# Two-operand vector work of GpSimd moved to VectorE in a transformer block

## The chip, the cores and the metric

The kernel runs on one core of a Trainium2 chip. A core has five engines that run their own queues of instructions in order and wait for each other by semaphores: TensorE (in the profile PE for its matmuls and PEld for its weight loads), VectorE (DVE), ScalarE (ACT), GpSimd (POOL) and SyncE (SP), which here only issues DMAs. The metric is the device time of one execution in microseconds (us); less is better.

## The reference

One layer of a hybrid encoder on a sequence of 1024 rows with 1024 features, in f32. A token mixer runs a short convolution and an attention without softmax side by side, merges them under two gates, and a squared-ReLU MLP of 4096 features follows.

```python
mod = c @ w_ada[l] + b_ada[l]
sh1, sc1, gt1, sh2, sc2, gt2 = jnp.split(mod, N_MOD, axis=-1)
h = modulate(rms_norm(x, g_pre_mix[l]), sh1, sc1)
proj = h @ w_in[l]
bg, cg, u, q, k, v, ga, gb = jnp.split(proj, split_pts, axis=-1)
y_conv = short_conv_branch(bg, cg, u, conv_w[l]) @ w_proj_conv[l]
o = stick_breaking_attention(q, k, v)       # 8 heads of 64
y_attn = o @ w_proj_attn[l]
merged = jax.nn.sigmoid(ga) * y_conv + jax.nn.sigmoid(gb) * y_attn
x = x + gt1[:, None, :] * rms_norm(merged @ w_out[l], g_post_mix[l])
h2 = modulate(rms_norm(x, g_pre_mlp[l]), sh2, sc2)
ff = jnp.square(jax.nn.relu(h2 @ w_mlp_in[l])) @ w_mlp_out[l]
x = x + gt2[:, None, :] * rms_norm(ff, g_post_mlp[l])
```

The attention weight of row t on row s < t is sigmoid(z_ts) times the product of 1 - sigmoid(z_tj) over the rows j between s and t: a running product from the diagonal to the left.

## The kernel before

**Numbers in two parts.** Every f32 operand of a large matmul is written as the sum of two numbers of a shorter type (fp32r), a high part and a low part. `split` (L101) makes them: ScalarE copies the operand into the high part, which rounds it (L103), and `sub` (L89, L90) subtracts the high part from the operand, on VectorE or on the engine that is handed in. A product is then three matmuls: high by high, high by low, low by high.

**Products of pairs.** The gates, both products of the MLP and their operands go through a seven-product scheme for 2 by 2 blocks (`pair_products`, L222, with the order 1, 2, 6, 5, 7, 3, 4 of L161). It needs sums and differences of the four blocks of each operand. For weights `side_s` (L163) makes four of them per pair of output columns, all on GpSimd, called from `pair_factors` (L207) with `nc.gpsimd` at L216; `parts` then splits each operand with VectorE for the low part. For activations the four blocks are turned into each other in place, step by step (L806 to L821 for the gates, `second_half`, L1099, for the MLP's first product).

**The stages**, in the order of time:

- The prologue (L373 to L536): x is normalised and turned, a part of the modulation and the value columns are computed. `value_rows` (L467) splits the 8 rows of the value weights with the low part on GpSimd.
- Attention and convolution (L552 to L788). For 8 heads and 4 pairs of row blocks, `weights_of` (L659) computes two sigmoids of the scores on ScalarE, clears the upper triangle of the diagonal block on GpSimd (L685), runs the product from the right as a scan on VectorE (L689), and multiplies both (L693). That multiplication is on GpSimd for the row blocks 0, 1, 2, 4 and 6 (widths 128, 256, 384, 640 and 896 columns) and on VectorE for 3, 5 and 7. `attend` (L702) then turns the weights on TensorE (L719), splits them (ScalarE and VectorE, tile `tu`) and multiplies by the values (L730); `finish` adds two halves (L740, tile `ot`). Between these, the projections for q, k and the convolution fill TensorE's time (L546); a string (L765) gives TensorE's order by hand: n for a step of weights, w for one of attending, f for one of filling.
- The gates (L794 to L897): operand sums over both parts of h, on an engine for each instruction by a string of p and v (L804), then 8 pairs of products with evictions on VectorE (L852) while the rest of the modulation is accumulated (L144).
- The two branch products (L962, L1001). `merged` (L983) multiplies by a gate on VectorE and adds the other branch on GpSimd (16 times, L986, by the string MERGED), then splits.
- The output product with residual and norms by blocks of 128 rows (L1042), with each block's columns turned and scaled into the MLP's operand. The last block's sums and low parts (`second_half`) follow an order string at L1229 in which a p sends an instruction to GpSimd: 15 of them.
- The MLP's first product: 16 pairs, `pair_products` with four weight sums each on GpSimd; results go to DRAM (`f_d`).
- The MLP's second product (L1266 to L1370): five groups of 2, 4, 4, 4 and 2 blocks, each with seven steps. `make` (L1186) forms a step's sums and both parts, two steps ahead of its matmuls (L1285): the sums of the weight side (64 in all) and the low parts of the weight side for odd blocks (56) on GpSimd, the rest on VectorE. `gather` (L1290) adds each result from PSUM into `ffacc` on VectorE (L1295). `finish_half` (L1329) scales the finished halves by a gain, 12 of 16 times on GpSimd, takes the norm, adds the residual and stores.

**The order.** In the prologue TensorE's and SyncE's queues, and in the attention TensorE's, are in the order of the code. All other queues are ordered by a planner when the program is built: it takes instructions as their inputs become ready by its own costs and prefers those that stand earlier in the code. Once built, each queue runs in order: an instruction that waits holds up what is behind it. SyncE issues all loads and stores.

Other work of GpSimd, which is not touched: memsets (among them L671), the powers -1/2 in `rstd_of` (L131), and the triangle (L685).

Of the kernel before, what the change touches and what calls it, by code (L numbers as in the profile page):

```python
# [30 lines left out]
def block_kernel(  # L31
# [19 lines left out]
    nc = tc.nc  # L51
# [132 lines left out]
    def sums_t(quads, i, k, eng=nc.vector):  # L184


        (q11, q12), (q21, q22) = quads[k]
        if i == 6:
            sub(q11, q12, q11, eng)
            sub(q12, q22, q12, nc.gpsimd)  # L190
            sub(q22, q22, q11, eng)
        else:
            sub(q21, q21, q22, nc.gpsimd)
# [13 lines left out]
    def pair_factors(raw, new_f, new_r):  # L207


        xs = {1: raw[0][:, :, :P], 2: raw[1][:, :, :P]}  # L210

        def split_of(i):
            if i not in xs:
                xs.update(side_s(
                    raw[0][:, :, :P], raw[1][:, :, :P], raw[0][:, :, P:], raw[1][:, :, P:],
                    new_f, nc.gpsimd,  # L216
                ))
            return parts(xs[i], lambda: new_r(i), nc.vector)

        return split_of  # L220
# [152 lines left out]
    with ExitStack() as es:  # L373
# [93 lines left out]
        def value_rows(k, n):  # L467
            raw = stage((P, n, CW))
            nc.sync.dma_start(
                raw, w_in[k * P : (k + n) * P, v0 : v0 + CW].rearrange("(a p) n -> p a n", p=P)  # L470
            )
            for i in range(n):
                hi, lo = wv[k + i] = tuple(
                    st.tile([P, CW], F32R, name=f"wv{w}{k + i}") for w in "hl"
                )
                split(raw[:, i, :], hi, lo, nc.vector if k + i in WV_DVE else nc.gpsimd)
# [43 lines left out]
        WV_DVE = set()  # L520
# [31 lines left out]
    with ExitStack() as es:  # L552
# [48 lines left out]
        def conv_taps(k):  # L601
            u = cv.tile([P, T + 2], F32, tag="cu", name=nm("cu"), bufs=1)
            y = uy[k]
            nc.gpsimd.memset(u[:, 0:2], 0.0)

            def use(half, ps):
                s = halves[half]
                nc.vector.tensor_tensor(
                    u[:, s.start + 2 : s.stop + 2], ps, y[:, s], op=ALU.mult
                )  # L610
                (nc.gpsimd if k in TAP else nc.vector).tensor_scalar(
                    y[:, s], u[:, s.start : s.stop], taps[:, k, 0:1], None, op0=ALU.mult
                )
                for j in (1, 2):
                    nc.vector.scalar_tensor_tensor(
                        y[:, s], u[:, s.start + j : s.stop + j], taps[:, k, j : j + 1], y[:, s],
                        op0=ALU.mult, op1=ALU.add,
                    )

            return use  # L620
# [38 lines left out]
        def weights_of(hd, i, out):  # L659
# [12 lines left out]
            for s0 in range(0, w, HALF):  # L672
# [11 lines left out]
                if s1 == w:  # L684
# [8 lines left out]
                    (nc.gpsimd if i in MUL else nc.vector).tensor_tensor(  # L693
# [65 lines left out]
        MUL = (0, 1, 2, 4, 6)  # L759
        TAP = ()  # L760
# [33 lines left out]
    with ExitStack() as es:  # L794
# [7 lines left out]


        engines = "pppvvpvpvpvp pvvpvppvpppv pvpvvvvppvpv vvpvvvvpvvpv"  # L804
        gate_on = on(engines)
        for k in range(4):  # L806
            q11, q12, q22, q21 = (gt.tile([P, HALF], F32, tag="e", name=nm("e"), bufs=8) for _ in range(4))
            quads.append([[q11, q12], [q21, q22]])
            for o, i, eng in zip((q11, q12, q22, q21), (1, 5, 3, 2), gate_on[k]):
                hi, lo = yop[i][k]  # L810
                add(o, f(hi), f(lo), eng)
            for (o, l, r), eng in zip(
                ((q11, q12, q11), (q12, q22, q12), (q22, q22, q11), (q21, q21, q22)), gate_on[k][4:]
            ):
                sub(o, l, r, eng)
            for i, eng in zip((6, 7, 4), gate_on[k][8:]):
                split_t(quads, yop, i, k, eng=eng)
        for _ in fill:
            pass
        for k in range(4):  # L820
            split_t(quads, yop, 5, k, eng=gate_on[k][11])  # L821
# [126 lines left out]
    MERGED = "pppppppppppppppp vvvvvvvvvvvvvvvv"  # L948
# [79 lines left out]
    with ExitStack() as es:  # L1028
# [70 lines left out]
        def second_half(step):  # L1099
# [4 lines left out]
            eng = nc.gpsimd if "p" in rest else nc.vector  # L1104
# [81 lines left out]
    def make(n):  # L1186

        g, i = steps[n]
        for j in range(GROUPS[g]):
            for side, o, a, b, op in SUMS.get(i, ()):  # L1190
                eng = nc.gpsimd if side == "x" else nc.vector
                o, a, b = (raw_of(r, j, side) for r in (o, a, b))
                eng.tensor_tensor(o, a, b, op=op)
        made[n] = []
        for j in range(GROUPS[g]):
            fs = []
            for side in "xy":
                to = factor_at(n, j, side)
                eng = nc.gpsimd if side == "x" and j % 2 else nc.vector
                split(raw_of(WHERE[side][i], j, side), *to, eng)  # L1200
# [25 lines left out]
    with ExitStack() as es:  # L1226
        def rest_of_h():
            order = """
                53ap 50a s50ap 51a 52a s51a n0 n1 51b 50b s52a s31 s30 52b 53b s53a 73ap 72ap 70p s33 s53b 60 s50b s52bp s32 71p 72bp 62p 73bp s51b 63 61 42p s62p 41p s63 s60 40a s42 s71 s61 43 40b s40p s70 s73 s43 s72p s41  # L1229
# [36 lines left out]
    with ExitStack() as es:  # L1266
# [56 lines left out]


        GAIN = "pppv pppv pppv pppv"
        SUM = "vvvv vvvv vvvv vvvv"
        AT = {(0, 0): 0, (1, 1): 1, (1, 0): 2, (0, 1): 3}

        def finish_half(b, q):  # L1329
# [14 lines left out]
            eng = nc.vector if GAIN.split()[b % 4][AT[b // 4, q]] == "v" else nc.gpsimd  # L1344
            eng.tensor_tensor(o, o, g2r[q], op=ALU.mult)
            if again:
                r = rstd_of(ss)
                for h in range(2):
                    o = acc[:, b, halves[h]]
                    if SUM.split()[b % 4][AT[b // 4, h]] == "v":  # L1350
                        nc.vector.scalar_tensor_tensor(
                            xt[h], o, r, xt[h], op0=ALU.mult, op1=ALU.add
                        )
                    else:
                        nc.scalar.activation(o, o, AF.Copy, scale=r)
                        add(xt[h], xt[h], o, nc.gpsimd)
# [46 lines left out]
```

## Time and profile before

| | |
|---|---|
| time, median of 3 runs | 1512.68 us |
| all runs | 1512.03, 1512.68, 1515.39 us |
| the profiled execution, its own time | 1514.89 us |
| its span, first to last instruction | 1513.2 us |
| mean granted TensorE clock | 0.968 |

The span is the time from the first to the last instruction that the profiler recorded; the little that the execution's own time has on top lies around it. In rows of the trace an instruction is named by engine, line, operation and out<-in of the tiles; a line can be that of a helper (L90 is every `sub`), so the tile names tell where it belongs: `y`, `g`, `h`, `fr` are slots of the MLP, `e`, `gy` and `t`, `s` the gates' operands and weights, `a` and `pt` the attention's weights, `cy` and `cu` the convolution's. "x78 | 79.5, 1058" means 78 instructions, 79.5 us busy in all, 1058 ns each on average; after it stands how long the engine idled just before them and which instruction ended that. Records of VectorE overlap a little, since the next one starts before the last one's record ends; the pace is read from start to start.

### The profile page before, as it was taken

How to read it: one execution, taken by the hardware profiler on the slowest of the kernel's cores; microseconds unless marked ns; L12 is line 12 of the kernel's file. 1: busy time of each engine (PE TensorE's matmuls, PEld its weight loads, DVE VectorE, ACT ScalarE, POOL GpSimd, SP SyncE). 2: the span in 40 equal slices, each digit the busy share in tenths (PEclk: the TensorE clock that was granted, in tenths of full speed). 3: DMA queues.
4: the chain of work that ended last, by engine and by line, in shares of the span. 5: the costliest groups of instructions: out<-in, count | busy, mean ns of one | idle time of the engine just before them, and what ended most of it. 6: DMA issues, size and time to landing. Idle time of an engine off the chain costs nothing.

```text
span 1513.2 us, 18030 instructions
## 1 busy us (share of the span) xinstructions
PE 1394.2 (92%) x6281; PEld 1131.0 (75%) x6281; DVE 1090.9 (72%) x1355; ACT 643.8 (43%) x1301; POOL 598.7 (40%) x516
## 2 busy tenths in 40 slices
PE   5999999999967998999999699999999699999976
PEld 4788778888855876788787478888887478787865
DVE  6737877877699665347546966555536988989988
ACT  5646656656324433413355433333323443343532
POOL 3214434434384332005104643333314645748365
PEclk9999999999988999999999799999999899999998
DMA  8501011111125566654413133333355225150224
GB/s 299 161 28 34 23 50 48 29 57 28 57 70 153 186 222 219 211 195 148 142 70 112 56 112 112 112 112 112 112 181 179 93 64 166 57 167 29 84 70 167
DMA packets 107567, 171.10 MB, mean 113 GB/s; under 512 B 7322, under 2 KB 66766, under 8 KB 107476
## 3 DMA queue, kind: packets, MB, share of 16 engines
q1 hardware_dynamic: 107476, 169.95, 34.2%
q8 instruction: 49, 0.80, 0.2%
q14 instruction: 42, 0.34, 0.1%
HBM read 132.16 MB, written 37.76 MB: 112 GB/s over the span
## 4 chain that ended last, share of the span: by engine, by line
PE 63%; DVE 19%; DMA 6%; issue 5%; ACT 4%; POOL 3%; SPq 0%; DVEq 0%; ACTq 0%; POOLq 0%
PE s L233 22%; PE s L1285 16%; PE mm L546 9%; DVE y L90 2%; PE s L120 2%; PE s L121 2%; PE s L122 2%; PE v L507 2%; PE o L730 2%; DVE pt L689 2%; PE tr L719 2%; DMA wa<-in_w_ada_dram 1%; DMA raw<-in_w_in_dram 1%; DVE acc L144 1%; DVE h L90 1%
## 5 line engine op out<-in xcount | busy, mean ns | idle before, releaser
L1285 PE MATMUL s<-y,y 128*128 128x512 f32 x984 | 242.1, 397 | 20.3 <-DVE y L90 13.6
L1285 PEld LDWEIGHTS s<-y,y 128*128 128x128 f32 x984 | 186.8, 191 | 65.5 <-DVE y L90 16.2
L546 PE MATMUL mm<-hTh,wh 128*128 128x512 f32 x320 | 128.9, 403 | 0.0
L546 PE MATMUL mm<-hTh,wl 128*128 128x512 f32 x320 | 125.4, 392 | 0.0
L546 PE MATMUL mm<-hTl,wh 128*128 128x512 f32 x320 | 125.4, 392 | 0.0
L685 POOL TENSOR_SCALAR_AFFINE_SELECT a<-a 128x128 f32<-128x128 f32 x64 | 64.0, 1002 | 143.4 <-ACT a L683 143.2
L103 ACT CAST y<-g 128x512 fp32r<-128x512 f32 x104 | 58.5, 619 | 131.6 <-PE s L1285 103.4
L233 PE MATMUL s<-hTh,t 128*128 128x512 f32 x256 | 89.1, 417 | 20.5 <-DVE cy L627 13.4
L689 DVE TENSOR_TENSOR_SCAN pt<-pt,dmask 128x128 f32<-128x128 f32 (+3 forms) x64 | 93.5, 1467 | 13.3 <-ACT pt L682 12.8
L1295 DVE TENSOR_TENSOR ffacc<-s,ffacc 128x512 f32<-128x512 f32 x124 | 81.3, 679 | 14.5 <-PE s L1285 14.3
L233 PE MATMUL s<-mTh,g 128*128 128x512 f32 x256 | 87.0, 404 | 3.8 <-ACT mTh L103 2.8
L90 DVE TENSOR_TENSOR y<-g,y 128x512 fp32r<-128x512 f32 x78 | 79.5, 1058 | 7.4 <-PE s L233 5.5
L233 PE MATMUL s<-mTh,h 128*128 128x512 f32 x240 | 80.7, 402 | 3.6 <-DVE h L90 2.5
L90 DVE TENSOR_TENSOR tu<-tr,tu 128x512 fp32r<-128x512 f32 (+2 forms) x112 | 54.9, 492 | 38.2 <-ACT tu L103 37.4
L103 ACT CAST tu<-tr 128x512 fp32r<-128x512 f32 (+2 forms) x112 | 49.0, 438 | 74.2 <-PE tr L719 51.2
L93 POOL TENSOR_TENSOR g<-raw,raw 128x512 f32<-128x512 f32 x16 | 24.2, 1510 | 140.7 <-PE s L233 128.2
L233 PEld LDWEIGHTS s<-hTh,t 128*128 128x128 f32 x256 | 50.9, 200 | 35.1 <-issue 14.6
L1285 PE MATMUL s<-fr,fr 128*128 128x512 f32 x288 | 74.2, 392 | 1.7 <-DVE fr L90 1.7
L233 PE MATMUL s<-y,g 128*128 128x512 f32 x288 | 72.0, 393 | 2.7 <-DVE y L90 2.3
L233 PE MATMUL s<-y,h 128*128 128x512 f32 x288 | 71.1, 391 | 0.0
L546 PEld LDWEIGHTS mm<-hTh,wl 128*128 128x128 f32 x320 | 60.1, 188 | 13.3
L90 POOL TENSOR_TENSOR y<-g,y 128x512 fp32r<-128x512 f32 x26 | 41.5, 1595 | 70.7 <-ACT y L103 70.7
(279 smaller groups left out, 3645.8 us busy)
## 6 DMA issues: line engine op xcount, KB each, us to landing
raw<-in_w_in_dram SPq DMA_DIRECT2D x38, 512.0 KB, 3.8
wa<-in_w_ada_dram SPq DMA_DIRECT2D x32, 512.0 KB, 4.1
raw<-in_w_mlp_in_dram SPq DMA_DIRECT2D x32, 512.0 KB, 3.9
g<-in_w_mlp_out_dram SPq DMA_DIRECT2D x40, 256.0 KB, 3.4
g<-f_d SPq DMA_DIRECT2D x40, 256.0 KB, 3.2
sg<-sg_d SPq DMA_DIRECT2D x16, 512.0 KB, 3.9
f_d<-wl SPq DMA_DIRECT2D x16, 512.0 KB, 5.1
f_d<-wh SPq DMA_DIRECT2D x16, 512.0 KB, 3.8
```

The lines of the kernel that those rows point to most:

```text
L90: eng.tensor_tensor(o, a, b, op=ALU.subtract)
L103: nc.scalar.copy(hi, src)
L120: nc.tensor.matmul(ps, lh, rh, start=i == 0, stop=False)
L121: nc.tensor.matmul(ps, lh, rl, start=False, stop=False)
L122: nc.tensor.matmul(ps, ll, rh, start=False, stop=i == n - 1)
L233: nc.tensor.matmul(ps, l, r, start=first and k == 0 and j == 0, stop=k == nk - 1 and j == 2, skip_group_check=True,)
L507: nc.tensor.matmul(vb[b], l, r, start=k == 0 and i == 0, stop=k == KC - 1 and i == 2, skip_group_check=True,)
L546: nc.tensor.matmul(ps, w[a][:, k, :], hT[b][:, k, s], start=k == 0 and i == 0, stop=k == KC - 1 and i == 2, skip_group_check=True,)
L685: nc.gpsimd.affine_select(a[:, i * P : w], a[:, i * P : w], pattern=[[-1, P]], compare_op=ALU.is_gt, fill=0.0, base=0, channel_multiplier=1,)
L689: nc.vector.tensor_tensor_scan(pt[:, 0:w][:, ::-1], pt[:, 0:w][:, ::-1], dmask[:, T - w : T][:, ::-1], 1.0, ALU.mult, ALU.max,)
L1285: nc.tensor.matmul(ps, l[:, s], r, start=start and j == 0 and n == 0, stop=j == len(fs) - 1 and n == 2, skip_group_check=True,)
L1295: nc.vector.tensor_tensor(o, ps, o, op=ALU.add)
```

## The change

All sums, low parts and products that GpSimd did are given to VectorE: 329 instructions. The strings and sets that chose an engine go away or lose their p; the order string at L1229 keeps its steps. Nothing else is added or taken out, and no buffer changes.

```diff
         if i == 6:
             sub(q11, q12, q11, eng)
-            sub(q12, q22, q12, nc.gpsimd)
+            sub(q12, q22, q12, eng)
...
                 xs.update(side_s(
                     raw[0][:, :, :P], raw[1][:, :, :P], raw[0][:, :, P:], raw[1][:, :, P:],
-                    new_f, nc.gpsimd,
+                    new_f, nc.vector,
                 ))
...
-                split(raw[:, i, :], hi, lo, nc.vector if k + i in WV_DVE else nc.gpsimd)
+                split(raw[:, i, :], hi, lo)
...
-                    (nc.gpsimd if i in MUL else nc.vector).tensor_tensor(
+                    nc.vector.tensor_tensor(
                         a[:, 0:w], a[:, 0:w], pt[:, 1 : w + 1], op=ALU.mult
                     )
...
-        engines = "pppvvpvpvpvp pvvpvppvpppv pvpvvvvppvpv vvpvvvvpvvpv"
-        gate_on = on(engines)
...
-            for o, i, eng in zip((q11, q12, q22, q21), (1, 5, 3, 2), gate_on[k]):
+            for o, i in zip((q11, q12, q22, q21), (1, 5, 3, 2)):
                 hi, lo = yop[i][k]
-                add(o, f(hi), f(lo), eng)
...
+                add(o, f(hi), f(lo), nc.vector)
+            for o, l, r in ((q11, q12, q11), (q12, q22, q12), (q22, q22, q11), (q21, q21, q22)):
+                sub(o, l, r, nc.vector)
+            for i in (6, 7, 4):
+                split_t(quads, yop, i, k)
...
-    MERGED = "pppppppppppppppp vvvvvvvvvvvvvvvv"
+    MERGED = "vvvvvvvvvvvvvvvv vvvvvvvvvvvvvvvv"
...
-            eng = nc.gpsimd if "p" in rest else nc.vector
+            eng = nc.vector
...
             for side, o, a, b, op in SUMS.get(i, ()):
-                eng = nc.gpsimd if side == "x" else nc.vector
                 o, a, b = (raw_of(r, j, side) for r in (o, a, b))
-                eng.tensor_tensor(o, a, b, op=op)
+                nc.vector.tensor_tensor(o, a, b, op=op)
...
                 to = factor_at(n, j, side)
-                eng = nc.gpsimd if side == "x" and j % 2 else nc.vector
-                split(raw_of(WHERE[side][i], j, side), *to, eng)
+                split(raw_of(WHERE[side][i], j, side), *to)
...
-            eng = nc.vector if GAIN.split()[b % 4][AT[b // 4, q]] == "v" else nc.gpsimd
-            eng.tensor_tensor(o, o, g2r[q], op=ALU.mult)
+            nc.vector.tensor_tensor(o, o, g2r[q], op=ALU.mult)
```

The choices at L611 (TAP was empty) and L1350 (SUM was all v) named VectorE already and only lose their branch. `sums_t` (L184), the first lines of the diff, is called by nothing in this kernel.

More of the change, by code (lines that the diff above doesn't have):

```diff
@@ L189, in sums_t @@
             sub(q11, q12, q11, eng)
-            sub(q12, q22, q12, nc.gpsimd)
+            sub(q12, q22, q12, eng)
             sub(q22, q22, q11, eng)
         else:
-            sub(q21, q21, q22, nc.gpsimd)
+            sub(q21, q21, q22, eng)
     def split_t(quads, yop, i, k, cols=slice(0, HALF), eng=nc.vector):
@@ L519, in block_kernel @@
         TURN_DVE = {(1, 0), (1, 1), (2, 1)}
-        WV_DVE = set()
         groups = {"A": (0, 1, 2, 3), "B": (4,), "C": (5, 6, 7), "a": (0, 1), "d": (2, 3), "b": (4,), "c": (5, 6, 7)}
@@ L610, in use @@
                 )
-                (nc.gpsimd if k in TAP else nc.vector).tensor_scalar(
+                nc.vector.tensor_scalar(
                     y[:, s], u[:, s.start : s.stop], taps[:, k, 0:1], None, op0=ALU.mult
@@ L758, in block_kernel @@
                 nc.scalar.copy(u[:, 0, :], dmask[:, :P])
-        MUL = (0, 1, 2, 4, 6)
-        TAP = ()
         units = [(hd, g) for hd in range(NH) for g in range(NB // 2)]
@@ L808, in block_kernel @@
             quads.append([[q11, q12], [q21, q22]])
-            for o, i, eng in zip((q11, q12, q22, q21), (1, 5, 3, 2), gate_on[k]):
+            for o, i in zip((q11, q12, q22, q21), (1, 5, 3, 2)):
                 hi, lo = yop[i][k]
-                add(o, f(hi), f(lo), eng)
[L812 to L817, printed above, removed]
+                add(o, f(hi), f(lo), nc.vector)
[3 more added lines that the diff above has]
+                split_t(quads, yop, i, k)
         for _ in fill:
@@ L820, in block_kernel @@
         for k in range(4):
-            split_t(quads, yop, 5, k, eng=gate_on[k][11])
+            split_t(quads, yop, 5, k)
         psm_es.close()
@@ L1228, in rest_of_h @@
             order = """
-                53ap 50a s50ap 51a 52a s51a n0 n1 51b 50b s52a s31 s30 52b 53b s53a 73ap 72ap 70p s33 s53b 60 s50b s52bp s32 71p 72bp 62p 73bp s51b 63 61 42p s62p 41p s63 s60 40a s42 s71 s61 43 40b s40p s70 s73 s43 s72p s41
+                53a 50a s50a 51a 52a s51a n0 n1 51b 50b s52a s31 s30 52b 53b s53a 73a 72a 70 s33 s53b 60 s50b s52b s32 71 72b 62 73b s51b 63 61 42 s62 41 s63 s60 40a s42 s71 s61 43 40b s40 s70 s73 s43 s72 s41
             """
@@ L1321, in block_kernel @@
         blocks = {}
-        GAIN = "pppv pppv pppv pppv"
-        SUM = "vvvv vvvv vvvv vvvv"
-        AT = {(0, 0): 0, (1, 1): 1, (1, 0): 2, (0, 1): 3}
         def finish_half(b, q):
@@ L1349, in finish_half @@
                     o = acc[:, b, halves[h]]
[L1350 to L1356, printed above, removed]
+                    nc.vector.scalar_tensor_tensor(
+                        xt[h], o, r, xt[h], op0=ALU.mult, op1=ALU.add
+                    )
                     nc.sync.dma_start(out[s, halves[h]], xt[h])
```

## The prediction, made before the changed kernel ran

> **What bounds the kernel now.** I read the page first, then the busy times by stage, then who TensorE waits for, then the order of time in the full stretches.
>
> ```profile
> span 1513.2 us, 18030 instructions
> PE 1394.2 (92%) x6281; PEld 1131.0 (75%) x6281; DVE 1090.9 (72%) x1355; ACT 643.8 (43%) x1301; POOL 598.7 (40%) x516
> ...
> PE 63%; DVE 19%; DMA 6%; issue 5%; ACT 4%; POOL 3%; SPq 0%; DVEq 0%; ACTq 0%; POOLq 0%
> ```
>
> TensorE is busy for 1394 of 1513 us: at most 119 us can be won, and VectorE, with 19% of the chain of waits, is the next to look at. The same by stage (length, then busy time and count of PE, PEld, DVE, ACT, POOL; clock, DMA share, GB/s):
>
> ```profile
> 0.00:84.00 84.00, 66.81 (x287) 52.87 (x288) 55.48 (x102) 47.34 (x96) 22.22 (x33) 0.92 0.64 207
> 84.00:410.00 326.00, 312.75 (x1677) 263.55 (x1677) 240.39 (x314) 188.72 (x416) 120.62 (x175) 0.99 0.13 39
> 410.00:480.00 70.00, 49.13 (x182) 37.53 (x181) 69.04 (x57) 18.52 (x33) 53.53 (x32) 0.83 0.31 94
> 480.00:830.00 350.00, 339.19 (x1488) 273.94 (x1487) 201.75 (x254) 142.79 (x291) 81.30 (x65) 0.99 0.50 170
> 830.00:867.00 37.00, 21.84 (x71) 15.18 (x69) 34.13 (x38) 16.11 (x35) 25.12 (x19) 0.77 0.15 45
> 867.00:1150.00 283.00, 282.46 (x1220) 228.98 (x1221) 156.95 (x207) 91.66 (x162) 88.99 (x58) 1.00 0.38 128
> 1150.00:1215.00 65.00, 48.65 (x189) 36.58 (x188) 62.45 (x63) 27.75 (x52) 41.23 (x27) 0.92 0.31 102
> 1215.00:1456.00 241.00, 236.86 (x1036) 194.05 (x1035) 223.58 (x260) 97.92 (x183) 139.53 (x88) 1.00 0.27 89
> 1456.00:1513.00 57.00, 36.49 (x142) 28.32 (x140) 47.19 (x67) 13.04 (x36) 26.13 (x23) 0.85 0.45 157
> ```
>
> Two kinds of stage. In 84 to 410, 480 to 830, 867 to 1150 and 1215 to 1456 TensorE is the bound; it idles 13.3, 10.8, 0.5 and 4.1 us there. In three transitions VectorE is full (69.0 of 70, 34.1 of 37, 62.5 of 65 us) and TensorE idles 20.9, 15.2 and 16.4 us: 52.5 us in 172. TensorE's own waits there name VectorE (total, times, longest):
>
> ```profile
> PE s L233 <- DVE cy L627: 13.4, 1, 13.4
> PE s L233 <- DVE t L90: 5.1, 3, 2.5
> ...
> PE s L1076 <- DVE wh L1066: 5.7, 1, 5.7
> ...
> PE s L1285 <- DVE y L90: 11.1, 5, 5.8
> ```
>
> So the change is judged by one question: does VectorE get through these transitions sooner when it also does GpSimd's share? VectorE's and GpSimd's orders of time from 1175.7 on answer it.
>
> ```profile
> 1191.07 1.75 DVE L90 TENSOR_TENSOR y<-g,y 128x512 fp32r<-128x512 f32 x1
> 1192.74 1.76 DVE L90 TENSOR_TENSOR y<-h,y 128x512 fp32r<-128x512 f32 x1
> ...
> 1199.61 0.68 DVE L1193 TENSOR_TENSOR h<-h,h 128x512 f32<-128x512 f32 x1
> 1200.22 0.68 DVE L90 TENSOR_TENSOR y<-g,y 128x512 fp32r<-128x512 f32 x1
> 1200.82 0.68 DVE L1193 TENSOR_TENSOR wl<-g,g 128x512 f32<-128x512 f32 x1
> ```
> ```profile
> 1190.56 1.71 POOL L1193 TENSOR_TENSOR h<-wh,h 128x512 f32<-128x512 f32 x1
> 1192.23 1.72 POOL L1193 TENSOR_TENSOR h<-h,h 128x512 f32<-128x512 f32 x1
> ```
>
> The two engines take turns. Beside GpSimd a VectorE instruction starts every 1.67 us (1191.07, 1192.74) and so does a GpSimd one; with GpSimd idle, the same form starts every 0.60 us (1199.61, 1200.22, 1200.82). A pair costs 1.67 us now and two VectorE instructions 1.20 us. **Doing the work in one place is 0.47 us a pair cheaper wherever both engines are full**; where VectorE has room it costs VectorE 0.60 us more and gives back up to 1.07 us of stretch. The groups by form show the same in their means: sums in SBUF are stretched where GpSimd is at work, not before.
>
> ```profile
> L90 DVE TENSOR_TENSOR y<-g,y 128x512 fp32r<-128x512 f32 x78 | 79.5, 1058 | 7.4 <-PE s L233 5.5 <-PE s L1285 1.3 <-ACT y L103 0.6
> ...
> L90 DVE TENSOR_TENSOR hTl<-tmp,hTh 128x512 fp32r<-128x512 f32 x8 | 5.5, 686 | 1.5 <-ACT hTh L493 1.3 <-ACT hTh L103 0.2
> ```
>
> **What is moved.** From the code: 8 low parts of the value rows, 40 products in the attention, 22 sums and low parts for the gates, 96 sums of weight halves (4 for each of 8 + 16 pairs), 16 merged sums, 15 steps of rest_of_h, 64 sums and 56 low parts of the last product, 12 gains: 329. GpSimd keeps 187 of its 516. No DMA is issued by a moved line; loads on SP's queue that wait for a raw tile are released when its sums are done, which comes no later. The terms, against the profiled execution:
>
> - **410 to 480, the gates' operands.** 57 + 32 instructions at 0.60 us are 53 us, and some 4 more for the accumulations of twice the width, which appear in this group:
>
> ```profile
> L144 DVE SCALAR_TENSOR_TENSOR acc<-wa,vcols,acc 128x1024 f32<-128x1024 f32 x32 | 49.0, 1532 | 22.8 <-DMA wa<-in_w_ada_dram 17.9 <-DMA acc<-in_b_ada_dram 4.8
> ```
>
>   57 us where 69.0 stand now: 12 less. TensorE's 20.9 us of idle time can take that up, but the casts of ScalarE stand between sums and low parts, and the planner may put more sums ahead of the product that ends the 13.4 us wait. I take -9, between -4 (a third) and -14.
> - **830 to 867, the last block's turn into the channel mixer.** 38 + 18 (one of the 19 is a power, which stays) at 0.60 are 33.6 us, no gain on 34.1; but some 20 of them, the column parts, have 128 or 384 columns, and a narrow one is short:
>
> ```profile
> L90 DVE TENSOR_TENSOR tu<-tr,tu 128x128 fp32r<-128x128 f32 x32 | 9.0, 281 | 1.8 <-ACT tu L103 1.7
> ```
>
>   With 0.3 us less for each it is 27.6. I take -4, between -1 and -9.
> - **1150 to 1215, the first group of the last product.** Its worst part:
>
> ```profile
> 1175.70:1197.80 22.10, 13.25 (x43) 10.02 (x44) 22.10 (x15) 11.59 (x23) 21.51 (x13) 0.77 0.10 31
> ```
>
>   Less the ones cut by its edges, 13 + 12 instructions: 15 us in place of 22.1, and TensorE idles 8.9 there. -7, between -3 and -10.
> - **1215 to 1456.** 260 + 88 at 0.60 are 209 us where 223.6 stand, under TensorE's 236.9: only its 4.1 us of idle time are to be had. -2, between -4 and 0.
> - **84 to 410, the attention.** Here GpSimd's products ran beside VectorE's scans, and the change puts them in between. Rows of the products, of one scan beside a product, and of the same scan in the first head, from the chain of waits, where no product was running (start and length):
>
> ```profile
> L693 DVE TENSOR_TENSOR a<-a,pt 128x1024 f32<-128x1024 f32 x8 | 9.7, 1208 | 0.0
> L693 DVE TENSOR_TENSOR a<-a,pt 128x768 f32<-128x768 f32 x8 | 7.6, 952 | 0.1
> ...
> L693 POOL TENSOR_TENSOR a<-a,pt 128x896 f32<-128x896 f32 x8 | 14.5, 1816 | 1.5 <-DVE pt L689 0.9
> ```
> ```profile
> 389.15 1.77 POOL L693 TENSOR_TENSOR a<-a,pt 128x896 f32<-128x896 f32 x1
> ```
> ```profile
> 389.78 3.29 DVE L689 TENSOR_TENSOR_SCAN pt<-pt,dmask 128x1024 f32<-128x1024 f32 x1
> ```
> ```profile
> 136.22 2.29 DVE pt L689
> ```
>
>   The scan took 3.29 us, 1.00 over the 2.29 of the first head's, and the product's end at 390.92 lies 1.14 behind its start: it waited for GpSimd. From 952 and 1208 (1 ns a column) the moved products of 128, 256, 384, 640 and 896 columns would take 0.31, 0.44, 0.57, 0.82 and 1.08 us: 3.2 a head, 26 in all, and VectorE goes from 240 to about 260 of 326 us. A product of 896 columns at 1.08 in front of the last scan is no worse than the 1.77 that it waits through now; the narrower ones had no such wait and are added. TensorE's waits that end at VectorE here:
>
> ```profile
> PE tr L719 <- DVE a L693: 5.4, 7, 1.5
> PE o L730 <- DVE ot L740: 4.3, 5, 1.7
> PE o L730 <- DVE tu L90: 2.5, 2, 2.3
> ```
>
>   14 places have no room. At some 0.2 us each, +3; between -3 (the scans' relief reaches the path and nothing else) and +26 (every product in full).
> - **The rest.** 0 to 84 (8 low parts), 867 to 1150 (TensorE 282.5 of 283 us, which hides all of it) and 480 to 830: 0, the last +-3. In the gate stage GpSimd's sums wait for their weights, a wait that VectorE would now stand in, with the evictions of L852 and the low parts queued behind:
>
> ```profile
> POOL s L93 <- DMA raw<-in_w_in_dram: 38.7, 4, 18.5
> ...
> DVE t L90 <- ACT t L103: 19.9, 14, 6.0
> ```
>
>   But the low part of the same tile stands ahead of the sums in the code and waits for the same load through ScalarE already; if that cover goes, the price is at most the longest wait of those low parts, 6.0 us, at each of the 4 places. 1456 to 1513: 12 gains at 0.60 against about as much stretch: -1, between -5 and +3.
>
> Sum: -9 - 4 - 7 - 2 + 3 - 1 = **-20 us**. The profiled execution took 1514.9 us (1513.2 of span and 1.7 around it): 1495. It lies 2.2 over the median of 1512.7, so the forecast is **1493**. With the small and the large ends of the terms together 1478 to 1509, as they will not all fall to one side.
>
> **Rivals.** (a) *The transitions empty.* If relief is passed on whole, the three lose 14 + 9 + 10 and the rest 4 + 3: -40, 1473. Against it: ScalarE's casts and the DMA waits stay. 0.08. (b) *Hidden.* The queue's order is remade by the planner, the products that TensorE waits for come behind as much work as now, and the relief falls where TensorE is full: within 3 us of 1513. For it: 0.5 us of idle time in 867 to 1150 shows how much relief buys nothing. 0.09. (c) *The attention goes to VectorE*, the slower case. One queue now holds scan, product, next scan and low parts; each of 32 units makes TensorE wait by the product's full price, 26 us at the transposes, and again at the low parts behind, up to 52. It decides from where the attention gives back over 23 us, 0.7 us a unit; in the middle, +39 - 23, 1529. For it: the 14 waits; against it: VectorE's room of 66 us there, and the scans' relief. 0.17. (d) *A stretched instruction stays stretched*, if 1.75 us is VectorE's own pace in a crowd. Then the moved work comes on top: 27 + 88 + 12 instructions from 1150 on at 0.60, +76, 1589. Against it: the 0.60 pitch follows in the very microseconds in which GpSimd pauses. 0.03. [...]
>
> **How the numbers follow.** Forecast 0.63, (a) 0.08, (b) 0.09, (c) 0.17, (d) 0.03. Faster than before by over 0.2% (3 us, about what a measurement of this kernel can tell from no change): forecast and (a), 0.71; within it (b), 0.09; slower (c) and (d), 0.20. The range holds forecast and (b), reaches to (a) and takes the near part of (c): 1474 to 1518.
>
> **What would show it.** Right: VectorE's 128x512 sums all near 0.68 us, its total busy time within 3% of 1091, a first transition shorter by some 9 us, the alternation of 1175 to 1198 gone, TensorE's idle time down to about 100 us, GpSimd under 120 us. Wrong: TensorE's waits on a L693, tu and ot above 20 us together; VectorE waiting for in_w_in loads in the gate stage; a wait on cy L627 that stays at 13 us, the planner's order then, not the pace, being its cause; 128x512 sums that stay over 1 us, by which the whole argument falls.

## The result, and the profile after

The changed kernel takes 1460.33 us (median of 4 runs, 1457.95 to 1463.91) where the kernel before takes 1512.88 beside it: a ratio of 0.9652, with a 95% interval of 0.9624 to 0.968. That is 52.5 us less; the prediction said 20 less, with a range that ended at 1474. The profiled execution of the changed kernel took 1457.99 us. It is a quick one of its kernel and that of the kernel before (1514.89) a slow one, so the two traces compared here lie 56.9 us apart, 4.4 more than the medians.

Its page, span, busy times and the shares of the chain of waits:

```profile
span 1456.3 us, 17855 instructions
...
PE 1374.5 (94%) x6281; PEld 1123.7 (77%) x6281; DVE 1076.1 (74%) x1684; ACT 645.2 (44%) x1301; POOL 95.8 (7%) x187
...
PE 76%; DVE 14%; DMA 3%; ACT 3%; issue 3%; POOL 1%; SPq 0%; DVEq 0%; ACTq 0%; POOLq 0%
```

Three things stand in it. VectorE runs 329 instructions more (1684 against 1355) and is busy for 15 us less. GpSimd fell from 598.7 to 95.8 us. And TensorE, with the same 6281 matmuls, is busy for 19.7 us less (1394.2 before): its work is unchanged, so it was done faster.

The same stages, cut at the same matmuls as those shown of before (length; busy time and count of PE, PEld, DVE, ACT, POOL; granted clock, DMA share, GB/s):

```profile
0.00:86.00 86.00, 66.72 (x287) 53.94 (x288) 54.13 (x110) 47.76 (x96) 10.69 (x25) 0.94 0.62 202
86.00:417.30 331.30, 315.68 (x1678) 264.49 (x1678) 254.66 (x354) 189.42 (x416) 64.58 (x135) 0.99 0.13 39
417.30:474.80 57.50, 43.06 (x182) 34.79 (x181) 55.61 (x88) 19.77 (x35) 0.00 (x0) 0.88 0.34 104
474.80:815.00 340.20, 333.18 (x1487) 271.29 (x1486) 209.34 (x308) 141.46 (x288) 13.48 (x19) 1.00 0.53 176
815.00:840.00 25.00, 18.82 (x71) 14.34 (x70) 22.88 (x45) 16.62 (x36) 1.54 (x1) 0.80 0.15 43
840.00:1122.00 282.00, 282.00 (x1220) 228.61 (x1219) 169.10 (x267) 94.44 (x165) 0.00 (x0) 1.00 0.38 128
1122.00:1172.40 50.40, 45.73 (x190) 36.17 (x190) 49.45 (x83) 26.12 (x51) 0.00 (x0) 0.97 0.46 154
1172.40:1408.60 236.20, 236.20 (x1035) 194.04 (x1034) 220.39 (x363) 98.59 (x184) 0.00 (x0) 1.00 0.30 97
1408.60:1456.30 47.70, 33.16 (x142) 26.04 (x140) 40.56 (x72) 11.04 (x32) 5.51 (x8) 0.94 0.42 150
```

Each row against its partner before splits the change into TensorE's idle time (length less PE) and its busy time:

| Stage (times of before) | Predicted term | Length | PE idle | PE busy |
|---|---|---|---|---|
| 0 to 84, prologue | 0 | +2.0 | +2.1 | -0.1 |
| 84 to 410, attention | +3 | +5.3 | +2.4 | +2.9 |
| 410 to 480, gates' operands | -9 | -12.5 | -6.4 | -6.1 |
| 480 to 830, gates and branches | 0 | -9.8 | -3.8 | -6.0 |
| 830 to 867, into the channel mixer | -4 | -12.0 | -9.0 | -3.0 |
| 867 to 1150, first MLP product | 0 | -1.0 | -0.5 | -0.5 |
| 1150 to 1215, last product's first group | -7 | -14.6 | -11.7 | -2.9 |
| 1215 to 1456, last product | -2 | -4.8 | -4.1 | -0.7 |
| 1456 to the end | -1 | -9.3 | -6.0 | -3.3 |
| Sum | -20 | -56.7 | -37.0 | -19.7 |

So there are two surprises. The second and the third transition emptied further than forecast (9.0 and 11.7 us of idle time where 4 and 7 were taken; the first gave 6.4 where 9 was taken), and so did the end. And one third of the difference is no idle time at all. The same rows show the clock granted higher (0.83 to 0.88, 0.77 to 0.80, 0.92 to 0.97, 0.85 to 0.94 in the three transitions and at the end), and the clock is most of it: wherever the two traces record a granted clock below 1.00 it is 0.50. These stretches add up to 95.4 us before, in which TensorE was busy for 63.0 us, and to 49.7 after, in which it was busy for 28.2. At half speed a matmul starts every 0.43 us, at full speed every 0.23, so the work takes about twice as long, and the 34.8 us less are worth 17.4 of the 19.7. In the first 84 us TensorE's busy time does not follow this (12.9 us of it at 0.50 before, 9.1 after, and 66.8 and 66.7 us in all); from there on the working gives 15.4 of 19.6.

What TensorE still waits for (total, times, longest):

```profile
PE s L233 <- ACT hTh L103: 14.3, 1, 14.3
PE tr L718 <- DVE a L692: 5.5, 8, 2.0
PE o L729 <- DVE ot L739: 5.1, 6, 1.9
...
PE s L1274 <- DVE ffacc L1284: 4.8, 4, 2.1
PE o L729 <- DVE tu L90: 4.6, 5, 2.9
...
PE s L1274 <- DVE y L90: 3.8, 2, 3.3
```

The 13.4 us gap behind the convolution's last matmuls is still there, now 14.3, with ScalarE's cast as the last to come instead of `cy`: VectorE is busy 55.6 of 57.5 us around it. VectorE's order of time has the convolution's last product near the end of the gap in both kernels, of before first:

```profile
442.23 0.68 DVE L627 TENSOR_TENSOR cy<-mm,cy 128x512 f32<-128x512 f32 x1
```
```profile
450.31 0.70 DVE L626 TENSOR_TENSOR cy<-mm,cy 128x512 f32<-128x512 f32 x1
```

Between the start of the gap and this product VectorE starts 9 instructions before (429.6 to 442.23 us) and 22 after (436.9 to 450.31). The pace has risen, and the planner has put that much more ahead of the product. The three waits of the attention grew from 12.2 to 15.2 us together. The waits on `y` and `ffacc` in the last product, 13.6 and 11.3 us over the whole span before, are 3.8 and 4.8.

The forms of VectorE's work that stood for the contention are back at the pace that they have alone:

```profile
L90 DVE TENSOR_TENSOR y<-g,y 128x512 fp32r<-128x512 f32 x104 | 67.9, 691 | 3.8 <-PE s L1274 2.0 <-PE s L233 1.2 <-ACT y L103 0.5
...
L688 DVE TENSOR_TENSOR_SCAN pt<-pt,dmask 128x1024 f32<-128x1024 f32 x8 | 18.5, 2312 | 0.0
```

The scan's line of before:

```profile
L689 DVE TENSOR_TENSOR_SCAN pt<-pt,dmask 128x1024 f32<-128x1024 f32 x8 | 23.4, 2927 | 1.5 <-ACT pt L682 1.3
```

The sum was at 1058 ns (now 691), the scan over 1024 columns at 2927 (now 2312). And where the two engines took turns, VectorE's order of time now reads:

```profile
1152.43 0.69 DVE L90 TENSOR_TENSOR y<-g,y 128x512 fp32r<-128x512 f32 x1
1153.03 0.70 DVE L1183 TENSOR_TENSOR wl<-g,g 128x512 f32<-128x512 f32 x1
1153.63 0.70 DVE L1183 TENSOR_TENSOR h<-h,wl 128x512 f32<-128x512 f32 x1
1154.24 0.70 DVE L1183 TENSOR_TENSOR h<-h,h 128x512 f32<-128x512 f32 x1
```

One starts every 0.60 us, without a break.

### The profile page after: what moved, and what is told of

Read it like the earlier page. It is cut to its first block, busy times and chain, and to the rows that moved or that the text cites. A ratio compares the mean times of both kernels' runs of the same rounds, so it can differ in the third digit from the quotient of the medians.

```text
span 1456.3 us, 17855 instructions
## 1 busy us (share of the span) xinstructions
PE 1374.5 (94%) x6281; PEld 1123.7 (77%) x6281; DVE 1076.1 (74%) x1684; ACT 645.2 (44%) x1301; POOL 95.8 (7%) x187
## 4 chain that ended last, share of the span: by engine, by line
PE 76%; DVE 14%; DMA 3%; ACT 3%; issue 3%; POOL 1%; SPq 0%; DVEq 0%; ACTq 0%; POOLq 0%
PE s L233 28%; PE s L1274 19%; PE mm L545 8%; PE s L120 4%; PE s L121 4%; PE s L122 4%; PE v L507 3%; DVE pt L688 2%; PE o L729 2%; DVE a L692 2%; PE tr L718 1%; DMA wa<-in_w_ada_dram 1%; DMA raw<-in_w_in_dram 1%; POOL a L684 1%; DVE tu L90 1%
## 5 line engine op out<-in xcount | busy, mean ns | idle before, releaser
L1274 PE MATMUL s<-y,y 128*128 128x512 f32 x984 | 236.8, 393 | 8.4 <-DVE ffacc L1284 3.9
L233 PE MATMUL s<-hTh,t 128*128 128x512 f32 x256 | 83.9, 398 | 14.4 <-ACT hTh L103 14.3
L688 DVE TENSOR_TENSOR_SCAN pt<-pt,dmask 128x128 f32<-128x128 f32 (+3 forms) x64 | 87.1, 1365 | 8.5 <-ACT pt L681 8.1
L131 POOL TENSOR_TENSOR rstd<-var,mhalf 128x1 f32<-128x1 f32 x32 | 23.1, 725 | 920.0 <-DVE var L128 919.9
L90 DVE TENSOR_TENSOR tu<-tr,tu 128x512 fp32r<-128x512 f32 (+2 forms) x112 | 55.1, 494 | 34.5 <-ACT tu L103 33.5
L90 DVE TENSOR_TENSOR y<-g,y 128x512 fp32r<-128x512 f32 x104 | 67.9, 691 | 3.8 <-PE s L1274 2.0
L545 PEld LDWEIGHTS mm<-hTh,wl 128*128 128x128 f32 x320 | 60.2, 188 | 13.4
L233 PEld LDWEIGHTS s<-hTh,t 128*128 128x128 f32 x256 | 48.6, 190 | 25.9 <-ACT hTh L103 14.6
L545 PEld LDWEIGHTS mm<-hTl,wh 128*128 128x128 f32 x320 | 60.5, 189 | 8.9
L545 PEld LDWEIGHTS mm<-hTh,wh 128*128 128x128 f32 x320 | 60.4, 189 | 8.8
```

Of the source, the lines that this page charges most:

```text
L90: eng.tensor_tensor(o, a, b, op=ALU.subtract)
L233: nc.tensor.matmul(ps, l, r, start=first and k == 0 and j == 0, stop=k == nk - 1 and j == 2, skip_group_check=True,)
L545: nc.tensor.matmul(ps, w[a][:, k, :], hT[b][:, k, s], start=k == 0 and i == 0, stop=k == KC - 1 and i == 2, skip_group_check=True,)
L688: nc.vector.tensor_tensor_scan(pt[:, 0:w][:, ::-1], pt[:, 0:w][:, ::-1], dmask[:, T - w : T][:, ::-1], 1.0, ALU.mult, ALU.max,)
L1274: nc.tensor.matmul(ps, l[:, s], r, start=start and j == 0 and n == 0, stop=j == len(fs) - 1 and n == 2, skip_group_check=True,)
```

## The experiments

The theory was: two engines that each read two tiles of SBUF, the core's memory for all tiles but TensorE's results, slow each other down (before, a VectorE instruction on two tiles started every 1.67 us beside GpSimd's and every 0.60 with GpSimd idle), the end of that relieves the stages that VectorE fills, and the lower clock is a consequence of TensorE's gaps. The rivals: one part of the change carries it all; the gain comes from a new order of the planner and not from the pace; the clock drifted for another reason.

**Each part alone, on the kernel before.** Four kernels, which together move all but the 8 low parts of the value rows, all timed beside the same runs of the kernel before (1516.04 us).

The attention's products:

```diff
-        MUL = (0, 1, 2, 4, 6)
+        MUL = ()
```

> The kernel before with only the 40 attention products on VectorE. The comparison of the two traces by the n-th matmul puts +5 us into the attention. Theory 1 (parts add up, each stage keeps what it gains or loses): 1518 us (1515 to 1521). Theory 2 (the planner remade the whole order, the stages' differences do not belong to their own edits): within 2 us of 1513, or a change outside the attention.

1523.36 us, ratio 1.0042 (1.0028 to 1.0056). This part alone is slower, by the waits that the whole change has too:

```profile
PE tr L719 <- DVE a L693: 5.5, 8, 2.0
PE o L730 <- DVE ot L740: 5.1, 6, 1.9
...
PE o L730 <- DVE tu L90: 4.6, 5, 2.9
```

They are the changed kernel's to the last digit. So the attention's price belongs to its products and to nothing else in the change.

The gates' operand sums and weight sums:

```diff
-        engines = "pppvvpvpvpvp pvvpvppvpppv pvpvvvvppvpv vvpvvvvpvvpv"
+        engines = "vvvvvvvvvvvv vvvvvvvvvvvv vvvvvvvvvvvv vvvvvvvvvvvv"
...
-    def pair_factors(raw, new_f, new_r):
+    def pair_factors(raw, new_f, new_r, side=nc.gpsimd):
...
-                    new_f, nc.gpsimd,
+                    new_f, side,
...
+                nc.vector,
```

> The kernel before with only the gates' operand sums and the gates' weight sums on VectorE. By the two traces the matmuls come 14 us sooner from 443 to 490 us and 6 us sooner by 615. Theory 1: 1493 us (1489 to 1497). Theory 2: over 1503. By the prediction's own term for this part (-9, nothing behind 480) it would be 1504.

1497.18 us, ratio 0.988 (0.9856 to 0.9904). The stage behind 410, and TensorE's wait in it:

```profile
410.00:466.00 56.00, 41.75 (x172) 33.97 (x171) 55.48 (x88) 19.60 (x35) 0.00 (x0) 0.85 0.32 102
```
```profile
PE s L233 <- ACT hTh L103: 14.2, 1, 14.2
```

VectorE does 88 instructions in 55.48 us, which is full, where it needed 69.0 us for 57 of its own beside 32 of GpSimd's. The long wait stays; what went is what stood behind it, the 5.1 us on `t` among it. Followed by its matmuls, of which the n-th is the same in both kernels, this run is 13 us ahead of before by 481 and 21 by 748: the later 8 us lie among the gates' products, a place that the prediction had put at 0.

The merged sums, the steps of `second_half` and the weight sums of the MLP's first product (with `pair_factors` as above):

```diff
-    MERGED = "pppppppppppppppp vvvvvvvvvvvvvvvv"
+    MERGED = "vvvvvvvvvvvvvvvv vvvvvvvvvvvvvvvv"
...
-            eng = nc.gpsimd if "p" in rest else nc.vector
+            eng = nc.vector
...
-        return pair_factors(raw, lambda: gslot(F32, (P, 4, P)), new)
+        return pair_factors(raw, lambda: gslot(F32, (P, 4, P)), new, nc.vector)
```

> The kernel before with only the merged sums, the 15 steps of the last block and the MLP's weight sums on VectorE. By the two traces: -2.5 us near 748, -12.5 from 830 to 867, -0.6 later. Theory 1: 1497 us (1493 to 1501). Theory 2: over 1505. The prediction's term was -4: 1509.

1501.11 us, ratio 0.9902 (0.9886 to 0.9918). It is 3.5 us ahead by 748, 4 by 830 and 16 by 867: 12 of it in the turn into the channel mixer, where TensorE's waits on `wh` at L1076 fell from 7.7 to 2.7 us over the whole span.

The last product (sums and low parts of the x side, gains):

```diff
-                eng = nc.gpsimd if side == "x" else nc.vector
+                eng = nc.vector
...
-                eng = nc.gpsimd if side == "x" and j % 2 else nc.vector
+                eng = nc.vector
...
-        GAIN = "pppv pppv pppv pppv"
+        GAIN = "vvvv vvvv vvvv vvvv"
```

> The kernel before with only the last product's weight sums, its low parts and the gains on VectorE. By the two traces: -14.8 us from 1150 to 1215, -4.7 to 1456, -9.5 after that. Theory 1: 1484 us (1480 to 1488). Theory 2: over 1495. The prediction's terms were -10: 1503.

1486.99 us, ratio 0.981 (0.9792 to 0.9827), the largest part: 15 us by 1214, 21 by 1457, 29 at the end. The last 8 to 9 are far more than the 1 that the prediction gave to the end. VectorE's order of time of the kernel before shows why:

```profile
1458.59 1.74 DVE L90 TENSOR_TENSOR g<-g,g 128x512 fp32r<-128x512 f32 x1
...
1463.56 0.69 DVE L1319 TENSOR_TENSOR g<-g,raw 128x512 f32<-128x512 f32 x1 [0.22 <-DMA g<-mod_d]
1464.17 4.07 DVE L1295 TENSOR_TENSOR ffacc<-s,ffacc 128x512 f32<-128x512 f32 x6
```

The operands of the last group were still being made in turns with GpSimd at 1458.59. Behind them stood two products with loaded rows (`g<-mod_d`), and behind those six accumulations that TensorE waited for: 7.0 us. The rows' load was issued only at 1458.70, as it waited for one of these low parts (26.7 us for `h` of L90 on SyncE's queue), but VectorE idled only 0.22 us for it; what held the accumulations up was the work ahead of them in VectorE's queue. In the changed kernel the load is issued at 1405.43, and TensorE's longest wait there is 2.1 us.

By the medians the four add up: +7.3 - 18.9 - 14.9 - 29.0 = -55.5 us of 1516, where the whole change, 0.9652 of 1516, gives -53. So no part carries it all, and within some 3 us none needs another.

**The contention put back.** The changed kernel with GpSimd given useless work on a tile that nobody reads, one instruction beside each of the 120 sums and low parts of the last product's x side. In the first kernel, shown here, it subtracts two SBUF tiles; in the second `shadow` is `nc.gpsimd.tensor_copy(scr, a)` and reads one.

```diff
+    scr = dmask.bitcast(F32)
+
+    def shadow(a, b):
+        nc.gpsimd.tensor_tensor(scr, a, b, op=ALU.subtract)
...
+                if side == "x":
+                    shadow(o, b)
...
+                if side == "x" and j % 2:
+                    shadow(raw_of(WHERE[side][i], j, side), f(to[0]))
```

> The changed kernel, in which GpSimd again does a subtraction beside each of the 120 sums and low parts of the last product that were moved, into a scratch tile that nobody reads. VectorE's own work is that of the changed kernel. Theory 1 (the two engines take turns at something shared when both read two tiles of SBUF): VectorE's 128x512 sums in SBUF of the last product go from 0.69 to 1.2 us and more on average, its idle room of some 25 us there is used up, and the time goes to between 1500 and 1580 us. Theory 3 (what the change gained is the planner's order and the shorter queue, GpSimd's work by itself costs VectorE nothing): within 6 us of 1460.

> As the run before, but GpSimd copies one tile into the scratch tile in place of subtracting two. If any work of GpSimd on tiles of 128x512 holds VectorE up, the sums go above 1.0 us again and the time above 1490; if it is the second tile that they share, the sums stay near 0.69 us and the time within 6 us of 1460.

With two tiles: 1537.82 us (2 runs), ratio 1.0157 (1.0133 to 1.0181), 77 us over the changed kernel though no engine waits for GpSimd's subtractions. With one tile: 1467.19 us (2 runs), ratio 0.9691 (0.9665 to 0.9716), 7 us over it, a little more than expected. VectorE's groups by form, two tiles first, then one tile, and GpSimd's own in each:

```profile
L90 DVE TENSOR_TENSOR y<-g,y 128x512 fp32r<-128x512 f32 x104 | 102.2, 1014 | 1.2 <-PE s L233 1.2
L1188 DVE TENSOR_TENSOR g<-g,g 128x512 f32<-128x512 f32 x40 | 40.0, 1020 | 0.0
...
L1293 DVE TENSOR_TENSOR ffacc<-s,ffacc 128x512 f32<-128x512 f32 x124 | 82.1, 679 | 1.4 <-PE s L1283 1.4
```
```profile
L90 DVE TENSOR_TENSOR y<-g,y 128x512 fp32r<-128x512 f32 x104 | 74.4, 748 | 1.2 <-PE s L233 1.2
L1188 DVE TENSOR_TENSOR g<-g,g 128x512 f32<-128x512 f32 x40 | 29.0, 746 | 0.1
```
```profile
L1180 POOL TENSOR_TENSOR dmask<-g,y 128x512 f32<-128x512 f32 x26 | 45.1, 1734 | 397.2 <-ACT y L103 389.0 <-issue 7.7
```
```profile
L1180 POOL COPY dmask<-g 128x512 f32<-128x512 f32 x60 | 87.4, 1456 | 306.3 <-DMA g<-in_w_mlp_out_dram 276.4 <-DVE g L1188 26.8
```

The number of GpSimd's instructions is the same in both, and so is their place in the code; what differs is the second tile and with it the operation, a copy in place of a subtraction, and that is worth 70 us. The 104 low parts of the first line alone keep VectorE busy for 102.2 us with two tiles and for 74.4 with one, where the changed kernel has 67.9. `ffacc`, which reads one of its two operands from PSUM, the memory of TensorE's results, stays at 679 ns beside either. This speaks against the rival by which the gain was a new order's: VectorE keeps all its work in both kernels, and with the contention put back the changed kernel loses more than the change had won. On VectorE's side it matters where the operands lie (beside the subtractions 1014 ns with two in SBUF, 679 with one in PSUM); on GpSimd's side, whether it copies one tile (748) or subtracts two (1014).

**The wait that stayed.** The changed kernel with the convolution's leftover steps put ahead of the gates' operand sums in the code, so that the convolution's end would not stand behind them:

```diff
+        for _ in fill:
+            pass
...
-        for _ in fill:
-            pass
```

> The changed kernel with the last steps of the convolution put ahead of the gates' operand sums in the code, so that the planner prefers them. The changed kernel still idles 14.3 us on TensorE at 437 us, behind the last product of the convolution, at unchanged pace 0.60 us on VectorE. Theory 1 with the planner's order as the cause of that wait: the product comes right after its matmuls, the gap goes to 2 to 6 us, and the time to between 1448 and 1455. If the wait is VectorE's amount of work instead, TensorE idles as long a little later: 1458 to 1463.

1459.44 us, ratio 0.9637 (0.9618 to 0.9656): no change that can be told apart, and the same wait.

```profile
PE s L233 <- ACT hTh L103: 14.3, 1, 14.3
```

The planner put VectorE's instructions into nearly the same order whatever the code's, so the run didn't make the case it was meant to make. It leaves open whether an order exists that closes this gap; it would have to put the last `cy` ahead of some of the 22 instructions above, and the work put off would still have to be done by a VectorE that is full there (55.6 of 57.5 us).

**The clock.** The changed kernel with pauses of TensorE put where it runs without a break at a clock of 1.00, three long ones or fifteen short ones. A pause is a turn (a transpose) on TensorE, its eviction by VectorE (a copy out of PSUM), 22 further VectorE instructions (none in the short ones), and a turn that waits for them. Shown are the long ones; the short ones' first window reads f f and then fifteen times d f f.

```diff
+        hold = at.tile([P, P], F32, name="hold")
+        nc.gpsimd.memset(hold, 0.0)
...
+        def stall():
+            while True:
+                ps = bank(psm, "mm")
+                nc.tensor.transpose(ps[:, :P], ident, ident)
+                nc.vector.tensor_copy(hold, ps[:, :P])
+                for _ in range(22):
+                    nc.vector.tensor_tensor(hold, hold, hold, op=ALU.max)
+                nc.tensor.transpose(ps[:, P : 2 * P], hold, ident)
+                yield
...
-            ffffffffffffffffffffffffffffffffnffffffnfffffff
+            ffffffffdffffffffdffffffffdffffffffnffffffnfffffff
```

> The changed kernel with three pauses of TensorE put into its first window of the attention, where TensorE is busy without a break at a granted clock of 1.00 (84 to 130 us). Each pause is a turn on TensorE, an eviction and 22 small VectorE instructions on one 128x128 tile, and a turn that waits for them: some 4 to 6 us. If a pause brings a lower clock behind it (clock theory): TensorE's idle time in the window rises by 12 to 18 us, its busy time by 5 to 15 us on top for the same matmuls, the granted clock of the window falls below 0.9, and the run takes 1460 + 17 to 33, about 1485. If the clock has nothing to do with pauses: idle time alone, busy time within 1.5 us, granted clock 0.98 or more, about 1475.

> The changed kernel with fifteen short pauses of TensorE in the same window, each a turn, one eviction and a turn that waits for it, some 1 us each, so about as much idle time in all as the three long ones. Clock theory with a threshold between about 1 and 4 us, as the gaps of the runs so far suggest: idle time up by 10 to 18 us, busy time within 2 us, granted clock at 1.00, 1460 + 10 to 18, about 1474. If any idle time lowers the clock in proportion to its sum: busy time up by as much as with the long pauses, 5 to 15 us, about 1485.

Long pauses: 1495.59 us, ratio 0.9865 (0.984 to 0.989). Short ones: 1474.67 us, ratio 0.973 (0.9703 to 0.9756). The stretch with the same 111 matmuls in the changed kernel, with long pauses and with short ones (there with 6 and 29 added turns among the counts):

```profile
84.50:109.00 24.50, 24.50 (x111) 20.32 (x110) 8.09 (x11) 9.65 (x18) 0.68 (x1) 1.00 0.08 22
```
```profile
81.70:141.60 59.90, 31.80 (x117) 24.98 (x116) 27.99 (x80) 9.61 (x18) 0.58 (x1) 0.74 0.03 9
```
```profile
84.50:122.70 38.20, 31.49 (x140) 22.18 (x139) 12.47 (x26) 9.60 (x18) 0.62 (x1) 1.00 0.05 14
```

The long pauses, 28.1 us of idle time in three, made the 117 matmuls take 31.8 us. At the full clock they take 24.5 and 6 turns at 0.24 (from the short pauses: 7.0 us for 29 of them) 1.5: 26. The other 6 us are the clock, and it can be seen where they fell, one row for the last part of each pause and the first work behind it:

```profile
93.00:103.00 10.00, 4.55 (x12) 3.59 (x13) 4.85 (x17) 0.00 (x0) 0.00 (x0) 0.50 0.00 0
...
110.30:120.30 10.00, 3.64 (x9) 2.92 (x10) 5.70 (x19) 0.01 (x1) 0.00 (x0) 0.50 0.17 49
...
127.30:137.40 10.10, 4.07 (x10) 3.25 (x11) 5.38 (x17) 0.03 (x1) 0.00 (x0) 0.50 0.00 0
```

12.3 us of work at 0.50, half of which is 6.1. TensorE's waits in the pauses, long ones and then short ones:

```profile
PE mm L768 <- DVE hold L767: 28.1, 3, 10.0
```
```profile
PE mm L768 <- DVE hold L765: 6.7, 15, 0.9
```

With the short pauses, at most 0.9 us each, the clock stays at 1.00 through 6.7 us of idle time, and all that is lost is idle time and turns. The pauses were longer than planned (9.4 us and not 4 to 6), so that the first run's time came out above what either theory had said; the clocks and the busy times tell the theories apart. So 9.4 us of idle time brought the clock of 0.50, and at most 0.9 us did not. In the kernel before a shorter wait has it behind it too: TensorE waits 1.98 us from 742.4 on, and half speed follows.

```profile
742.40:745.30 2.90, 0.92 (x10) 0.93 (x9) 1.86 (x5) 1.06 (x5) 0.84 (x2) 1.00 0.39 151
745.40:748.80 3.40, 3.40 (x10) 2.63 (x9) 1.41 (x2) 3.40 (x11) 0.15 (x1) 0.50 0.71 259
```

No fixed bound comes out of these traces: a wait of 2.13 us near the end of the changed kernel (1436.8) has 1.00 behind it, and the stretch at 0.50 from 540.6 to 544.0 before follows on 10 us in which TensorE waited 0.2 us only.

**A version that keeps the attention as it was.** The changed kernel with the attention's products and the value rows' low parts back on GpSimd:

```diff
-                split(raw[:, i, :], hi, lo)
+                split(raw[:, i, :], hi, lo, nc.gpsimd)
...
-                    nc.vector.tensor_tensor(
+                    (nc.gpsimd if i in MUL else nc.vector).tensor_tensor(
...
+        MUL = (0, 1, 2, 4, 6)
```

> The changed kernel with the 40 attention products and the 8 low parts of the value rows back on GpSimd. By the two traces these are the only parts that lost: +2.0 us in the first 84 us and +5.3 by 410. Theory 1: 1453 us (1450 to 1456). Theory 2: within 2 us of 1460.

1456.75 us, ratio 0.9622 (0.9603 to 0.9641). Since that overlaps the spread of the changed kernel, it was run again beside it:

> The version with the attention's products and the value rows' low parts back on GpSimd, a second time and beside the changed kernel. If the attention's price of 6 us is a real loss of the change, it comes out 3 to 6 us below the changed kernel with intervals that part: about 1455 against 1460. If the 5 us that it lost between 1090 and 1178 are of the order that the planner makes and belong to it, 1 to 3 us and no parting of the intervals.

> The changed kernel as it is, a second time, for the comparison: 1460, ratio 0.964 to 0.966.

1456.02 us, ratio 0.9607 (0.9586 to 0.9629), against 1458.99 us, ratio 0.9628 (0.9605 to 0.9651). It is the fastest here by 3 us, and the intervals overlap, so that a gain is not shown. On the same matmul it is some 8 us ahead of the changed kernel's second run from 420 to 1090 and gives back 4 of them in the last product's first group, which the change back doesn't touch. The stretch there, of the changed kernel's second run and of this one:

```profile
1122.00:1180.00 58.00, 53.28 (x223) 42.50 (x223) 56.59 (x94) 31.00 (x58) 0.00 (x0) 0.97 0.43 148
```
```profile
1122.00:1180.00 58.00, 51.46 (x205) 39.76 (x204) 58.00 (x98) 28.48 (x54) 0.00 (x0) 0.94 0.36 119
```

The second kernel is ahead in time and yet gets 18 matmuls fewer done here, behind a VectorE that is full in both. That the planner, which lays out the whole program anew, chose another order here is argued from this, not shown.

## Why the prediction was right and wrong

Right were the direction and the mechanism by which idle time went. **The pace:** 0.60 us from start to start beside an idle GpSimd, in the transitions as in the last product; rival (d), by which a stretched instruction stays stretched, is refuted by the group means and by the two contention runs. **The load:** VectorE's busy time within 3% of 1091 (1076.1), GpSimd under 120 us (95.8), the alternation gone. **The attention:** +5.3 us against +3, of which +2.4 is idle time, at the waits named; rival (c) was the right place, at a seventh of its price (5.3 us against 39). **867 to 1150:** -1.0. **1215 to 1456:** -4.8, just past its end of -4: the whole idle time went, and 0.7 us of busy time.

**410 to 480** is right in part by luck: -12.5 lies within -4 to -14, but the term was meant as idle time, of which 6.4 us went where 9 was taken, and the other 6.1 are busy time. There one of the prediction's signs of being wrong came true: the wait of 13.4 us stayed. The prediction named the planner's order as the cause in that case, and the order of time agrees (22 instructions ahead of the last `cy` in place of 9); no run with another order showed it.

Wrong was the size, in three steps.

1. *"At most 119 us can be won", TensorE's idle time.* The ceiling and each term took TensorE's 1394 us as fixed. They weren't: 19.7 of the 56.7 us came out of them, the largest piece that the sum lacked. The page showed it all along in the windows, as a granted clock of 0.77 to 0.92 in just the stages with long gaps, and the prediction quoted those rows without a price for that column. TensorE's work at 0.50 fell from 63.0 to 28.2 us, worth 17.4 of the 19.7 (15.4 of 19.6 from 84 us on). The long pauses put in by hand (9.4 us each, with 0.50 over the 3.6 to 4.6 us of work behind) show that a gap can bring the lower clock; that the gaps of the kernel before, most of them shorter, brought its half speed is argued from their order in time, and one stretch, at 540.6, has no gap ahead of it. The other 2 to 4 us are unexplained.
2. *The terms of the transitions, where only part of the stage was priced.* For 1150 to 1215 the prediction put 25 instructions of the worst 22 us at 0.60 and nothing for the other 43 us. Its own rule over the whole stage is 63 + 27 instructions at 0.60 or 54 us, and with the 83 that it has now 50, which is what VectorE took (49.45); TensorE's idle time fell by 11.7 where 7 was taken. For 830 to 867 it took 4 of the 6.5 us that its own count gave; VectorE needs 22.9 us where 27.6 was worked out, as 45 instructions and not 56 stand there now, and idle time fell by 9.0.
3. *The zeros.* 480 to 830 was put at 0 within 3 as TensorE is the bound there; it held 10.8 us of idle time, of which 3.8 went, and with busy time 9.8 us: three stretches of 3.4 us at 0.50, in which TensorE was busy throughout (from 540.6, 605.5 and 745.4), are gone in this execution, worth 5.1 of the 6.0. 1456 to the end was put at -1 from its 12 gains alone, since their lines were the only moved ones that belong to it; -9.3 came, out of its range, because the last operands' turns with GpSimd reached into it and held up six accumulations (6.0 of idle time), and as 6.8 us of work at 0.50 are at 1.00 now (3.4). In the other direction 0 to 84 was put at 0 and lost 2.0; the version with the value rows' low parts back on GpSimd was 3.4 us ahead by 64. That is no proof of their price: two kernels with the prologue of before came out 1.5 and 1.6 us ahead of it there, and the changed kernel's second run 1.8 ahead of its first.

Over the whole span TensorE's idle time went to 81.8 us, where the prediction expected about 100. Rival (a), the emptied transitions, is the nearest: it gave -40 and 1473, and idle time alone fell by 37.0. That it comes so near is partly luck, as its three transitions gave 27.1 of its 33 and the end, which it did not name, 6.0. It stood at 0.08 on the ground that ScalarE's casts and the DMA waits stay. They do stay (14.3 us on `hTh`), but that is one gap, not all.

## What to carry to other kernels

Before moving work to a second engine, look at the mean of the same instruction with that engine idle and at work: a pair that takes longer than two in a row on one engine (here 1.67 us against 1.20) is a loss wherever both are full. When a stage is bound by such an engine, price all instructions of the stage at the new pace, not its worst part, and look for what they release behind the stage's end. And when gaps of TensorE go, count the clock too: its busy time at a granted clock under 1.00 is not fixed (here 63.0 us before and 28.2 after).

## What the runs showed that was not expected

- A pause of TensorE can cost more than itself: with 9.4 us of idle time comes a stretch of some 10 us at a clock of 0.50 that begins inside the pause and holds over the first 3.6 to 4.6 us of work behind it, 2 us lost each time. Fifteen pauses of up to 0.9 us cost nothing beyond their length and their added turns.
- The scatter between the changed kernel's four runs goes with the clock: they took 1457.95 and 1457.99 us at mean clocks of 0.982 and 0.983, and 1462.66 and 1463.91 at 0.976.
- GpSimd copying one tile beside VectorE's sums stretches them from 691 to 748 ns on average; subtracting two tiles, to 1014.
